# One pair of input chunks moved from chunk-wise products to block products, and the block-product pairs dealt out in another order

## The chip, the cores and the metric

The kernel runs on one core of a Trainium2 chip. The metric is the time of one execution on the device, in microseconds (us). Each kernel is executed several times and the median is given. One execution is taken by the hardware profiler; its records are called the trace here, and the page made from them the profile. Engines are named as in the profile: PE is the matrix engine (TensorE), PEld its weight loads, DVE VectorE, ACT ScalarE, POOL GpSimd, SP SyncE, which here only issues transfers. A difference of less than about 0.3% is not told from none.

## What is computed

One layer of a hybrid decoder trunk in float32, for 1024 positions and 1024 channels. The part of the reference that matters here:

```
h = rms_norm(x, g_mix)
z = einsum("bsd,de->bse", h, w_in) + b_in
va, ga, xb, gb, sa, sb = split(z)            # widths 1024 1024 1536 1536 1024 1024

u = va * sigmoid(ga)
u = causal_depthwise_conv(u, conv_a_w, conv_a_b)      # 31 taps
y_a = silu(layer_norm(u)) @ w_a_out

v = causal_depthwise_conv(xb, conv_b_w, conv_b_b)     # 4 taps
v = rg_lru(v, ...)                                    # gates by 16 heads, then a scan
y_b = (v * gelu(gb)) @ w_b_out

x = x + (sigmoid(sa) * y_a + sigmoid(sb) * y_b) @ w_o
x = x + square(relu(rms_norm(x, g_mlp) @ w_1)) @ w_2
return rms_norm(x, g_final)
```

## The kernel before

The 7168 output channels of `z` are 56 chunks of 128: VA and GA (8 each), XB and GB (12 each), SA and SB (8 each). All matmuls are float32 products made of three passes on 128x512 tiles: each operand is split into a high and a low part (`h`, `l`), and high by high, high by low and low by high are added up.

**First part (lines 735 and 836 to 897).** The list `CH` (line 694) names the chunks that are computed directly: 28 of them, all of VA, GA and XB. A chunk is 48 matmuls over the normalized input (`chunk_mm`). One loop runs over the chunks; at each step `s` it issues the load of the weights of chunk `s + 2`, the matmuls of chunk `s`, what follows from chunk `s - 1` (a bias and a convolution of XB, or `u_out`, which takes the sigmoid of GA on ACT and multiplies it by VA on DVE), and the weight splits of the next chunk (`split_w`: high part on ACT, low part by a POOL transfer that adds up). In between stand the head products of the recurrence (`head_mm`, tiles `rg`) and its scans in four groups (`scan_exp`, `scan_in`, `scan_root`, `scan_tile`), and the 31 taps of the convolution over each `u` (`conv`), which DVE does whenever it has nothing that is due. A finished convolution is stored (`yd`) and later summed over the eight tiles by POOL transfers (`ysum`).

Towards its end this part also prepares the second one: sums and differences of the four quarters of the input (`x_load`, `x_sum`, `x_parts`, lines 669 to 692), read back from a DRAM copy `xu`, and the first weights (`z_load`, tiles `zw`).

**Second part (lines 925 to 1063).** GB, SA and SB are computed in pairs of chunks. The input is cut into 2 x 2 blocks (channels by positions), the weights of a pair likewise, and seven block products give the four output blocks instead of eight (`z_mm`, 12 matmuls each, line 933). `ZPAIRS` (line 739) lists the 14 pairs: six of GB, four of SA, four of SB. `zseq` (line 785) gives the order of the products; the first two pairs are woven together, the others follow at seven products each. For each product a weight operand `zo` is made four products ahead (`z_lhs`: ACT and DVE, or ACT and a POOL transfer) from a block of `zw` or from a sum of blocks (`z_sums`, tiles `zs`). Behind the products stand the moves between banks (`z_post`) and the outputs (`z_out`): gelu on ACT for GB and a product with the scan's result `hb`, which goes to DRAM; a sigmoid on ACT for SA and SB, stored as `gates`.

**The rest.** `y_b`, layer norm, `y_a` and the output projection follow, in which the row statistics `x1_sums` and `x1_spread` use small banks of their own. Then the up projection by block products: the steps `gu` (line 1297) and `f` (line 1591) are woven by the table `GX` (line 1678), by numbered steps; the copy `u_late` (line 1351) takes the first sums of `gu4` and `gu5` out of their banks (`gu4a`, `gu5a`) before TensorE adds to them again. Last is the down projection (line 1903). All orders are fixed when the program is built: a list of clocks `clk` per engine is kept by hand (`at`, `later`, `vector_work`), and each engine runs its instructions in the order in which they were written.

Of the kernel before, what the change touches and what calls it, by code (L numbers as in the profile page):

```python
# [15 lines left out]
P = 128  # L16
# [15 lines left out]
def trunk_kernel(ctx: ExitStack, tc: tile.TileContext, x, xt_in, xt_eo, vecs, w_in, w_a_out, w_b_out,  # L32
# [87 lines left out]
    ep = stage.enter_context(tc.tile_pool(name="extra", bufs=1))  # L120
# [285 lines left out]
    xu = dp.tile([2, 4, P, S], F32, name="xu")  # L406
# [75 lines left out]
    def xb_parts(t):  # L482
        if t % 3 == 2:
# [67 lines left out]
    def scan_exp(g):  # L551
        at("A", 1.28)
        for t in range(3 * g, 3 * g + 3):
# [29 lines left out]
    def u_out(j, psv, psg):  # L583

        u = T(f"u{j}")
        uv = u.rearrange("p (o n) -> p o n", o=2)
        nc.scalar.activation(uv, psg.rearrange("p (n o) -> p o n", o=2), AF.Sigmoid,
                             bias=bin_c[:, GA + j:GA + j + 1])
        later(at("A", 1.11), 1.28, nc.vector.scalar_tensor_tensor, uv,
              psv.rearrange("p (n o) -> p o n", o=2), bin_c[:, VA + j:VA + j + 1], uv,  # L590
              ALU.add, ALU.mult)
        ut[j] = u
        fresh.append(j)
# [73 lines left out]
    xq = {}  # L667

    def x_load(c2):

        xq[c2] = {n: ep.tile([P, S], F32, tag="e", name=f"xs{n}_{c2}") if (n, c2) == (21, 0) else T(f"xs{n}_{c2}")
                  for n in (11, 12, 22, 21)}
        for n, a in xq[c2].items():
            nc.sync.dma_start(a, xu[n % 10 - 1, 2 * (n // 10 - 1) + c2])

    def x_sum(c2, ready):
        q = xq[c2]
        for n, a, b in ((11, 12, 11), (12, 22, 12), (22, 22, 11), (21, 21, 22)):
            later(ready, 1.2, nc.vector.tensor_tensor, q[n], q[a], q[b], ALU.subtract)

    def x_parts(c2, *ps):
        for p in ps:
            src = xq[c2][{6: 22, 7: 12, 5: 11, 4: 21}[p]]
            xbh[p][c2] = h = T(f"xs{p}h_{c2}", F32R)
            xbl[p][c2] = l = T(f"xs{p}l_{c2}", F32R)
            if c2 == 0 and p < 6:
                split_dma(src, h, l)
                at("A", 2.0)
            else:
                nc.scalar.activation(h, src, AF.Copy)  # L690
                later(at("A", 1.0), 1.2, nc.vector.tensor_tensor, l, src, h.bitcast(F32),
                      ALU.subtract)

    CH = [XB, VA, GA, XB + 1, XB + 2]
    for js, g in (((1,), 1), ((2,), 2), ((3,), 3), ((4, 5, 6, 7), 4)):
        CH += [c for j in js for c in (VA + j, GA + j)]
        CH += [XB + t for t in range(3 * g, min(3 * g + 3, 12))]
# [41 lines left out]
    ZPAIRS = [GB + 2 * i for i in range(6)] + [SA + 2 * i for i in range(4)]  # L739
    ZPAIRS += [SB + 2 * i for i in range(4)]  # L740
# [4 lines left out]
    def z_load(i, kk):  # L745

        zraw[i, kk] = raw = qp.tile([P, 2, 4, P], F32, tag="p", name=f"zw{i}_{kk}", bufs=4)
        c = ZPAIRS[i]
        nc.sync.dma_start(raw, w_in[c:c + 2, :, 4 * kk:4 * kk + 4, :].rearrange("m p k c -> p m k c"))
# [18 lines left out]

    def z_lhs(i, p):
# [12 lines left out]
        zo[i, p] = o  # L782
# [19 lines left out]
    HS0 = [4 + 5 * (n // 4) + n % 4 for n in range(NH)]  # L802
# [8 lines left out]
    for c2 in range(4):  # L811
        nc.sync.dma_start(xu[1, c2], xc[4 + c2])
    w_parts(3)
    with tc.manual_schedule(engines=ENGINES):
        for s in range(3, NC1):
            w_load(s + 2)
            if s in XL:
                x_load(XL[s])
# [19 lines left out]
            if before is not None:  # L838

                head_gate(before, 0, begun)  # L840
                head_mm(before, 1)
            if s > 3:
                chunk_mm(s, 18, 24)
            if new is not None:
# [3 lines left out]
            if c >= XB:  # L848
                xb_out(c - XB, zps[s - 1])
            elif c >= GA:  # L850
# [14 lines left out]
            for d in range(6):  # L865
                if s - d in EXP:
                    g = EXP[s - d]
                    lag = int(g < 3)
# [9 lines left out]
                    if 3 * g <= t < 3 * g + 3 and t < 11:  # L878
                        later(rooted[t], 4.8, scan_tile, t)
            if s == NC1 - 1:  # L880
                z_get(0, z_lhs)
                z_get(1, z_lhs)
            if s - 1 in XL:
                x_sum(XL[s - 1], max((r for r, *_ in todo), default=0))
            for f, *a in XS.get(s, ()):
                f(*a)
            if s == NC1 - 3:
                for i in range(4):
                    z_load(i // 2, i % 2)
            if s == 3:  # L890
                for c2 in range(4):
                    nc.sync.dma_start(xu[0, c2], xc[c2])
# [45 lines left out]
    def z_out(i, m_, hf, src, name):  # L938
        ci = ZPAIRS[i] + m_
        bias = bin_c[:, ci:ci + 1]  # L940
        if ci < SA:
# [17 lines left out]

    hb = {}  # L960

    def z_h(i, m_, hf):
        t = ZPAIRS[i] + m_ - GB
        if t < 12:
# [32 lines left out]
    ZX = {0: ((x_parts, 1, 7),), 7: ((later, 0, 4.8, scan_tile, 11),), 2: ((x_parts, 1, 5),), 4: ((x_parts, 1, 4),)}  # L997
    H_AT = {2: (0, 0), 5: (1, 1), 3: (0, 1), 4: (1, 0)}
    with tc.manual_schedule(engines=ENGINES):
# [40 lines left out]
        u_out(7, zps[NC1 - 2], zps[NC1 - 1])  # L1040
        x_parts(1, 6)
        vector_work(clk["V"])
        z_h(0, 0, 0)
        for n in range(len(zseq) + 2):
# [5 lines left out]
            taps["hold"] = n < 2  # L1050
# [372 lines left out]
    def x1_sums():  # L1423

        rst["ps"] = ps = bank("ssm")
# [48 lines left out]
    def x1_root(o):  # L1474
# [4 lines left out]
        if o == 0:  # L1479
            nc.vector.tensor_scalar(v, rst["ps"][:, 0:4], 1.0 / D, EPS, ALU.mult, ALU.add)  # L1480
# [19 lines left out]
    def x1_spread(o):  # L1500

        rd, rbk[o] = rbk[o], bank(f"rbm{o}")
# [146 lines left out]
    def g_get(n, f):  # L1649
# [500 lines left out]
```

## Time and profile before

| | |
|---|---|
| median of 3 runs | 1546.58 us (1546.01 to 1550.48) |
| profiled execution | 1546.4 us, span 1544.3 us, clock of TensorE 0.998 |
| first part, chunks from 42.63 us | until 360.62 us |
| second part, block products | from 360.62 us until about 630 us |
| last stage, down projection | from 1226.44 us |

The span is what the trace covers of the profiled execution. Starts are counted from its beginning. A row of the timeline gives start, length, engine, line, operation, output and input tiles with their shapes, and in brackets the idle time in front of it with the instruction that ended it. Matmuls overlap: one lasts 0.39 us in the trace, but the next starts 0.2267 us after it. A row of the order of instructions (fences in the next section) has the line, the operation, output and input tile, with numbers that tell tiles of one name apart.

### The profile page before, as it was taken

What the parts mean: (1) busy time and instruction counts of PE and PEld (TensorE: products, weight loads), DVE (VectorE), ACT (ScalarE), POOL (GpSimd) and SP (SyncE); (2) the same over time, 40 slices, a digit from 0 to 9 for tenths busy, and PEclk for the clock granted to TensorE, in tenths of its full rate; (3) what the DMA queues carried; (4) which work ended last, traced back from release to release, by engine and by line L of the source; (5) the groups of instructions that cost most, each with busy time, mean ns of one, the idle gap of its engine ahead of it and who ended that gap; (6) DMA issues with size and microseconds to landing.
All of it is one profiled execution on the core that took longest, in us unless ns stands there. A gap on an engine that the chain in (4) does not pass through costs nothing.

```text
span 1544.3 us, 19039 instructions
## 1 busy us (share of the span) xinstructions
PE 1533.0 (99%) x6777; PEld 1261.0 (82%) x6777; DVE 1218.4 (79%) x1643; ACT 903.5 (59%) x1258; POOL 188.6 (12%) x226
## 2 busy tenths in 40 slices
PE   9999999999999999999999999999999999999998
PEld 7878888788888888888888887888888888888886
DVE  6999989999899983468568878765555558888897
ACT  6748677576657657435275777444444475555553
POOL 0000000002222222000022332000000001111110
PEclk9999999999999999999999999999999999999999
DMA  8653654678999889854579897523333779888852
GB/s 348 169 127 94 161 139 134 155 229 218 263 263 260 196 204 259 278 191 122 185 198 302 192 195 190 205 80 134 116 114 109 242 205 228 224 224 223 206 125 109
DMA packets 132815, 294.18 MB, mean 190 GB/s; under 512 B 20848, under 2 KB 38896, under 8 KB 132720
## 3 DMA queue, kind: packets, MB, share of 16 engines
q1 hardware_dynamic: 101184, 213.00, 41.1%
q0 software_dynamic: 31392, 79.71, 28.2%
q8 instruction: 53, 0.87, 0.2%
q14 instruction: 42, 0.34, 0.1%
q10 hardware_dynamic: 144, 0.26, 0.1%
HBM read 152.93 MB, written 58.72 MB: 137 GB/s over the span
## 4 chain that ended last, share of the span: by engine, by line
PE 98%; DMA 1%; DVE 0%; ACT 0%; issue 0%; DVEq 0%; SPq 0%; POOL 0%; POOLq 0%
PE z L735 18%; PE d L1903 15%; PE yb L1121 8%; PE e L2020 3%; PE keep L1903 2%; PE z L258 2%; PE rg L530 1%; PE rg L532 1%; PE rg L531 1%; DMA zo<-zs 1%; PE gu5a L1297 0%; PE go2e L1297 0%; PE z5a L933 0%; PE gu3a L1297 0%; PE gu1a L1297 0%; PE go0e L1297 0%
## 5 line engine op out<-in xcount | busy, mean ns | idle before, releaser
L735 PE MATMUL z<-xh,win_h 128*128 128x512 f32 x400 | 124.8, 390 | 0.0
L735 PE MATMUL z<-xl,win_h 128*128 128x512 f32 x400 | 123.4, 389 | 0.0
L1915 DVE TENSOR_TENSOR acc<-acc,d 128x1024 f32<-128x1024 f32 x72 | 87.9, 1220 | 33.3 <-PE d L1903 32.7
L735 PE MATMUL z<-xh,win_l 128*128 128x512 f32 x400 | 99.4, 391 | 0.0
L735 PEld LDWEIGHTS z<-xh,win_l 128*128 128x128 f32 x400 | 75.1, 188 | 16.9
L735 PEld LDWEIGHTS z<-xh,win_h 128*128 128x128 f32 x400 | 75.0, 188 | 16.6 <-ACT win_h L68 0.4
L648 DVE SCALAR_TENSOR_TENSOR y<-u,vec,y 128x511 f32<-128x511 f32 (+14 forms) x120 | 88.5, 737 | 0.0
L735 PEld LDWEIGHTS z<-xl,win_h 128*128 128x128 f32 x400 | 75.1, 188 | 15.8
L648 DVE SCALAR_TENSOR_TENSOR yt<-u,vec,yt 128x511 f32<-128x511 f32 (+6 forms) x112 | 82.7, 738 | 0.0
L648 DVE SCALAR_TENSOR_TENSOR y<-yt,csum,y 128x511 f32<-128x511 f32 (+6 forms) x112 | 82.7, 738 | 0.0
L542 ACT ACTIVATE g<-rg,vec 96x1024 f32<-96x1024 f32 x32 | 35.6, 1113 | 79.6 <-PE rg L532 79.5
L1579 ACT ACTIVATE o<-s 128x512 fp32r<-128x512 f32 x58 | 34.7, 623 | 51.7 <-DVE s L1564 31.0
L67 POOL DMA_DIRECT2D win_l<-win_raw x25 | 21.6, 865 | 318.9 <-ACT win_l L66 248.4
L476 DVE SCALAR_TENSOR_TENSOR v<-xb,vec,v 128x1023 f32<-128x1023 f32 (+2 forms) x36 | 46.2, 1282 | 11.4 <-ACT v L467 10.4
L67 POOL DMA_DIRECT2D zo<-zw x42 | 36.2, 862 | 133.1 <-ACT zo L66 126.2
L1121 PE MATMUL yb<-hgh,wb_h 128*128 128x512 f32 x168 | 51.7, 389 | 0.0
L1121 PE MATMUL yb<-hgl,wb_h 128*128 128x512 f32 x168 | 51.7, 389 | 0.0
L66 ACT ACTIVATE zo<-zw 128x512 fp32r<-128x512 f32 x42 | 26.3, 626 | 31.0 <-DMA zw<-in_w_in_dram 8.9
L67 POOL DMA_DIRECT2D db_1l<-wr x7 | 6.0, 860 | 309.9 <-ACT db_1l L66 287.3
L1121 PE MATMUL yb<-hgh,wb_l 128*128 128x512 f32 x168 | 41.0, 389 | 0.0
L1085 DVE TENSOR_TENSOR o<-s,o 128x512 fp32r<-128x512 f32 x58 | 38.8, 683 | 0.0
L1121 PEld LDWEIGHTS yb<-hgh,wb_h 128*128 128x128 f32 x168 | 31.5, 188 | 6.6
(1795 smaller groups left out, 4667.5 us busy)
## 6 DMA issues: line engine op xcount, KB each, us to landing
w_raw<-in_w_dram SPq DMA_DIRECT2D x36, 512.0 KB, 5.6
fr<-fd SPq DMA_DIRECT2D x32, 512.0 KB, 6.0
wr<-in_w_dram SPq DMA_DIRECT2D x32, 512.0 KB, 6.1
zw<-in_w_in_dram SPq DMA_DIRECT2D x28, 512.0 KB, 6.1
win_raw<-in_w_in_dram SPq DMA_DIRECT2D x25, 512.0 KB, 4.1
win_l<-win_raw POOLq DMA_DIRECT2D x25, 512.0 KB, 4.5
zo<-zw POOLq DMA_DIRECT2D x42, 256.0 KB, 5.7
gates<-zg SPq DMA_DIRECT2D x32, 256.0 KB, 3.9
```

The lines of the kernel that those rows point to most:

```text
L67: nc.gpsimd.dma_start(l, src, accum_op=ALU.add)
L258: nc.tensor.matmul(z0[i][:, HALVES[hf]], w0[i][w][:, k, :], xpart(a, hf, k), start=k == 0 and which == "hh", stop=k == 7 and which == ("hl ...
L476: nc.vector.scalar_tensor_tensor(v[:, d:S], a[:, 0:S - d], cbw_c[:, w * 12 + t:w * 12 + t + 1], v[:, d:S], ALU.mult, ALU.add)
L542: nc.scalar.activation(a, gps.pop((n, gi))[:HD, :], AF.Sigmoid, bias=(ba_c, bx_c)[gi][:, n:n + 1])
L648: nc.vector.scalar_tensor_tensor(o[:, k:], a[:, 0:HS - k], c, o[:, k:], ALU.mult, add)
L735: nc.tensor.matmul(zps[s][:, HALVES[hf]], w[:, k, :], xw[k][part][hf], start=n == 0, stop=n == 23)
L1085: tt(l, src, h.bitcast(F32), ALU.subtract)
L1121: nc.tensor.matmul(ps[hf], a, b[:, HALVES[hf]], start=n == 0, stop=n == len(todo) - 1)
L1579: nc.scalar.activation(o[:, 0], src, AF.Copy)
L1903: nc.tensor.matmul(o, a, b, start=n == 0 and (p != 1 or g == 0), stop=n == len(todo) - 1, skip_group_check=p == 1 and g > 0)
L1915: tt(acc[p, q2], acc[p, q2], ps, ALU.add)
L2020: nc.tensor.matmul(o, a, b, start=n == 0 and t < 7, stop=n == len(todo) - 1, skip_group_check=t == 7)
```

## The change

One pair of chunks, VA 7 and GA 7, leaves the first part and becomes the pair `u7` of the second part. So `CH` has 26 chunks and is written out, its last two in the order GA 6, VA 6: the sigmoid of GA 6 is taken while VA 6 is multiplied, for which `u_out` is cut into `u_gate` and `u_value`. The pairs, 15 now, are dealt out: two SA, three GB, two SA, `u7`, three GB, four SB. `z_branch` and `z_joined` make `u7` out of the pair's four output blocks, and only then its convolution can begin.

The sums of the input quarters are no longer read back and made at the end of the first part. They are made in place in its steps 4 to 7 (`x_sum`), split or left whole (`x_make`), and stored in `xsd`. Before and early in the second part they are loaded (`x_get`, `x_raw`), and those left whole are split there (`x_split`, products 2, 3, 6 and 7). The last group of scans starts two steps ahead of the part's end, and its three tiles are scanned at the products 1, 4 and 9 of the second part; taps are held back for six products there instead of two. The first weights of the second part are loaded at step 24 of the 26. The low part of a `zo` is made on DVE for all products once the convolutions are over. In `GX` the operands for product 7 of `gu` come a step later, those for product 3 in one step. `x1_sums` uses the bank `rbm0` of the first `x1_spread`. Tiles of one small pool (`extra`) go to others.

The core of the diff:

```diff
-    CH = [XB, VA, GA, XB + 1, XB + 2]
-    for js, g in (((1,), 1), ((2,), 2), ((3,), 3), ((4, 5, 6, 7), 4)):
...
+    NJ = 7
+    CH = [XB + 0, VA + 0, GA + 0, XB + 1, XB + 2, VA + 1, GA + 1, XB + 3, XB + 4, XB + 5, VA + 2, GA + 2, XB + 6, XB + 7, XB + 8, VA + 3, GA + 3, XB + 9, XB + 10, XB + 11, VA + 4, GA + 4, VA + 5, GA + 5, GA + 6, VA + 6]
...
-    ZPAIRS = [GB + 2 * i for i in range(6)] + [SA + 2 * i for i in range(4)]
-    ZPAIRS += [SB + 2 * i for i in range(4)]
+    ZPAIRS = [{"u": lambda i: (VA + i, GA + i)}.get(
+        t[0], lambda i, c={"g": GB, "s": SA, "t": SB}.get(t[0]): (c + 2 * i, c + 2 * i + 1))(int(t[1]))
+        for t in "s0 s1 g0 g1 g2 s2 s3 u7 g3 g4 g5 t0 t1 t2 t3".split()]
...
-        if p in (7, 5):
+        if p in (7, 5) or conv_over():
...
-    EXP = {head_slot: g for g, head_slot in enumerate(HS0[4 * g + 3] + 1 for g in range(4))}
-    XL = {23: 0, 25: 1}
-    XS = {25: ((x_parts, 0, 6),), 26: ((x_parts, 0, 7, 5),), 27: ((x_parts, 0, 4),)}
+    EXP = {head_slot: g for g, head_slot in enumerate(HS0[4 * g + 3] + 1 for g in range(3))}
+    RAW = (4, 5)
+    XS = {4: ((x_sum, 0),), 5: ((x_make, 0, 5), (x_make, 0, 7)), 6: ((x_make, 0, 6), (x_make, 0, 4), (x_sum, 1)),
+          7: tuple((x_make, 1, p) for p in (5, 7, 6, 4)),
+          NC1 - 3: ((scan_exp, 3),), NC1 - 2: ((x_get, 0, 6), (x_get, 1, 6)),
+          NC1 - 1: ((scan_in, 0, 9, 10, 11), (scan_root, 3), (x_get, 0, 7), (x_get, 1, 7))}
...
-        if ci < SA:
+        if ci < XB:
+            z_branch(ci, hf, src, bias)
+        elif ci < SA:
...
+    def z_branch(ci, hf, src, bias):
+        j = ci % GA
+        if j not in zu:
+            zu[j] = T(f"u{j}")
+        d, g = halved(zu[j], hf), src.rearrange("p (n o) -> p o n", o=2)
+        if ci >= GA:
+            zg[j, hf] = g
+            nc.scalar.activation(src, src, AF.Sigmoid, bias=bias)
+            ready = at("A", 0.62)
+            if hf == 0:
+                later(ready, 0.63, nc.vector.tensor_tensor, d, d, g, ALU.mult)
+                z_joined(j)
+        elif hf == 0:
+            nc.scalar.activation(d, g, AF.Identity, bias=bias)
+            at("A", 0.62)
+        else:
+            later(0, 0.68, nc.vector.scalar_tensor_tensor, d, g, bias, zg.pop((j, hf)), ALU.add, ALU.mult)
+            z_joined(j)
...
-    ZX = {0: ((x_parts, 1, 7),), 7: ((later, 0, 4.8, scan_tile, 11),), 2: ((x_parts, 1, 5),), 4: ((x_parts, 1, 4),)}
+    ZX = {0: ((x_raw, 0, 5), (x_raw, 1, 5)), 1: ((later, 0, 4.8, scan_tile, 9),), 2: ((x_split, 0, 5),), 3: ((x_split, 1, 5),),
+          4: ((later, 0, 4.8, scan_tile, 10), (x_raw, 0, 4), (x_raw, 1, 4)), 6: ((x_split, 0, 4),), 7: ((x_split, 1, 4),),
+          9: ((later, 0, 4.8, scan_tile, 11),)}
...
-            taps["hold"] = n < 2
+            taps["hold"] = n < 6
...
-        8: ((g_parts, "u", 7, 0),), 9: ((up_lhs, 0, 7), (g_parts, "u", 7, 1), (up_lhs, 1, 7)),
-        10: ((g_parts, "u", 3, 0), (g_t, "u", 0, 4)),
-        11: ((g_parts, "u", 3, 1), (g_t, "u", 1, 4))}.items()})
+        9: ((g_parts, "u", 7, 0), (up_lhs, 0, 7)), 10: ((g_parts, "u", 7, 1), (up_lhs, 1, 7)),
+        11: ((g_parts, "u", 3, 0), (g_t, "u", 0, 4), (g_parts, "u", 3, 1), (g_t, "u", 1, 4))}.items()})
```

What the order of instructions shows at the places that matter. First PE in the up projection, where `f1b` (a bank of the step `f`) and the second addition to the bank `gu4a` meet; before:

```order
L1591 MATMUL f0b_8097<-gu6h1_7947,o0_6_7922 128x512
L1591 MATMUL f1b_8115<-gu6h0_7913,o1_6_7956 128x512
L1591 MATMUL f1b_8115<-gu6l0_7914,o1_6_7956 128x512
L1591 MATMUL f1b_8115<-gu6h0_7913,o1_6_7956 128x512 x2
L1591 MATMUL f1b_8115<-gu6l0_7914,o1_6_7956 128x512
L1591 MATMUL f1b_8115<-gu6h0_7913,o1_6_7956 128x512
L1591 MATMUL f1b_8115<-gu6h1_7947,o1_6_7956 128x512
L1591 MATMUL f1b_8115<-gu6l1_7948,o1_6_7956 128x512
L1591 MATMUL f1b_8115<-gu6h1_7947,o1_6_7956 128x512 x2
L1591 MATMUL f1b_8115<-gu6l1_7948,o1_6_7956 128x512
L1591 MATMUL f1b_8115<-gu6h1_7947,o1_6_7956 128x512
L1297 MATMUL gu4a_8003<-gu2h0_7653,gu4_2_7943 128x512
```

and of the change:

```order
L1635 MATMUL f0b_8117<-gu6h1_7967,o0_6_7942 128x512
L1635 MATMUL f1b_8135<-gu6h0_7933,o1_6_7976 128x512
L1635 MATMUL f1b_8135<-gu6l0_7934,o1_6_7976 128x512
L1635 MATMUL f1b_8135<-gu6h0_7933,o1_6_7976 128x512 x2
L1635 MATMUL f1b_8135<-gu6l0_7934,o1_6_7976 128x512
L1341 MATMUL gu4a_8023<-gu2h0_7673,gu4_2_7963 128x512
```

Gu4a now comes after 5 matmuls of f1b, not after all 12. Its other 11 follow, then the 12 of gu5a, and only then the 7 left of f1b; before, gu5a stood behind 9 matmuls of f0c.

The same place on ACT: `f11` is an output of `gu`, `gu7h` a high part for product 7, `o` a weight operand of `f` made of the sum `s3` of DVE, and `u1_late` the copy for which gu4a and gu5a wait. Before:

```order
L1356 ACTIVATE f11_3_7999<-gu3a_7846 128x512
L1239 ACTIVATE gu7h0_8016<-x1010_7493 128x1024
L1351 ACTIVATE u1_late_8020<-gu4a_8003 128x512
L66 ACTIVATE o0_7_8037<-s3_0_8035 128x512
L68 ACTIVATE o0_7_8037<-s3_0_8035 128x512
L1239 ACTIVATE gu7h1_8041<-x1011_7529 128x1024
L66 ACTIVATE o1_7_8046<-s3_1_8044 128x512
L68 ACTIVATE o1_7_8046<-s3_1_8044 128x512
L1351 ACTIVATE u1_late_8020<-gu5a_8022 128x512
```

and of the change:

```order
L1400 ACTIVATE f11_3_8019<-gu3a_7866 128x512
L1395 ACTIVATE u1_late_8036<-gu4a_8023 128x512
L1283 ACTIVATE gu7h0_8051<-x1010_7514 128x1024
L66 ACTIVATE o0_7_8056<-s3_0_8054 128x512
L68 ACTIVATE o0_7_8056<-s3_0_8054 128x512
L1395 ACTIVATE u1_late_8036<-gu5a_8038 128x512
L1283 ACTIVATE gu7h1_8074<-x1011_7550 128x1024
```

Between f11 and the second u1_late stand one gu7h and two `o` where there were two and four, and nothing stands ahead of the first.

Last the queue of SP at the end of the first part: `hd` are scan results on their way out, `win` raw weights of a chunk, `xs` and `xb` sums of the input, `zw` raw weights of the first two pairs. Before:

```order
L577 DMA hd_446<-g1_8_1974 128x1024
L61 DMA win26_raw_2595<-in_w_in_dram 128x1024
L656 DMA yd_447<-y3_2071 128x1024
L61 DMA win27_raw_2678<-in_w_in_dram 128x1024
L674 DMA xs11_1_2680<-xu_445 128x1024
L674 DMA xs12_1_2681<-xu_445 128x1024
L674 DMA xs22_1_2682<-xu_445 128x1024
L674 DMA xs21_1_2683<-xu_445 128x1024
L749 DMA zw0_0_2745<-in_w_in_dram 128x2x512
L749 DMA zw0_1_2747<-in_w_in_dram 128x2x512
```

and of the change:

```order
L61 DMA win25_raw_2494<-in_w_in_dram 128x1024
L577 DMA hd_443<-g1_8_1972 128x1024
L764 DMA zw0_0_2638<-in_w_in_dram 128x2x512
L764 DMA zw0_1_2640<-in_w_in_dram 128x2x512
L764 DMA zw1_0_2642<-in_w_in_dram 128x2x512
L764 DMA zw1_1_2644<-in_w_in_dram 128x2x512
L698 DMA xb6h_0_2646<-xsd_442 128x1024
L698 DMA xb6l_0_2648<-xsd_442 128x1024
L698 DMA xb6h_1_2650<-xsd_442 128x1024
L698 DMA xb6l_1_2652<-xsd_442 128x1024
L698 DMA xb7h_0_2732<-xsd_442 128x1024
```

The zw loads stand straight behind hd of tile 8, ahead of the sums; before, two chunk weights, a convolution's result and four sums stood in between.

More of the change, by code (lines that the diff above doesn't have):

```diff
@@ L403, in trunk_kernel @@
                 first_z(i, 1, k, "lh")
-    xu = dp.tile([2, 4, P, S], F32, name="xu")
+    xsd = dp.tile([4, 2, 2, P, S], F32, name="xsd")
     def first_scale(i):
@@ L549, in trunk_kernel, with scan_exp @@
     at_, rooted = {}, {}
-    def scan_exp(g):
-        at("A", 1.28)
-        for t in range(3 * g, 3 * g + 3):
+    def scan_exp(g, part=range(3)):
+        if 0 in part:
+            at("A", 1.28)
+        for t in (3 * g + n for n in part):
             r = gate[0, t]
@@ L665, in trunk_kernel @@
         xbh[p], xbl[p] = [None, None], [None, None]
[L667 to L692, printed above, removed]
@@ new lines, in trunk_kernel, with x_store, x_get, x_raw @@
+    stored = []
+    def x_store():
+        for a in stored:
+            nc.sync.dma_start(*a)
+        stored.clear()
+    def x_get(c2, p):
+        for n, a in enumerate((xbh, xbl)):
+            a[p][c2] = T(f"xb{p}{'hl'[n]}_{c2}", F32R)
+            nc.sync.dma_start(a[p][c2].bitcast(F32), xsd[p - 4, c2, n])
+    def x_raw(c2, p):
+        xbl[p][c2] = T(f"xb{p}l_{c2}", F32R)
+        nc.sync.dma_start(xbl[p][c2].bitcast(F32), xsd[p - 4, c2, 0])
+    def x_split(c2, p):
+        xbh[p][c2], l = T(f"xb{p}h_{c2}", F32R), xbl[p][c2]
+        nc.scalar.activation(xbh[p][c2], l.bitcast(F32), AF.Copy)
+        later(at("A", 1.06), 1.2, nc.vector.tensor_tensor, l, l.bitcast(F32), xbh[p][c2].bitcast(F32),
+              ALU.subtract)
@@ L767, in z_sums, with conv_over @@
             S_(4, z_blk(i, 0, 1), zs[i, 2], ALU.subtract)
+    def conv_over():
+        return not (ut or fresh or taps["wait"] or taps["now"] or taps["next"])
     def z_lhs(i, p):
@@ L1423, in x1_sums @@
     def x1_sums():
-        rst["ps"] = ps = bank("ssm")
+        rbk["row"] = ps = bank("rbm0")
         for n in range(4):
@@ L1500, in x1_spread @@
     def x1_spread(o):
-        rd, rbk[o] = rbk[o], bank(f"rbm{o}")
+        rd, rbk[o] = rbk[o], rbk["row"] if o == 0 else bank(f"rbm{o}")
         for i in range(4):
```

84 lines of the change are left out of this document (48 added, 36 removed).

## The prediction

> **What bounds the kernel now.** First the head of the page: the span, the busy time of the engines, and by which engine the chain that ended last was held.
>
> ```profile
> span 1544.3 us, 19039 instructions
> PE 1533.0 (99%) x6777; PEld 1261.0 (82%) x6777; DVE 1218.4 (79%) x1643; ACT 903.5 (59%) x1258; POOL 188.6 (12%) x226
> PE 98%; DMA 1%; DVE 0%; ACT 0%; issue 0%; DVEq 0%; SPq 0%; POOL 0%; POOLq 0%
> ```
>
> TensorE is busy for 99% of the span and is 98% of the chain. So the time is the number of matmuls by their spacing, and the stalls. The spacing is read from the chain in order of time, in its runs of one line:
>
> ```profile
> 42.63 21.76 PE z L735 x96
> ...
> 470.19 2.72 PE z6a L933 x12
> 472.92 2.72 PE z6f L933 x12
> ...
> 478.36 2.72 PE z6b L933 x12
> ```
>
> Two chunks of the first part (2 x 48 matmuls) are one row of 21.76 us, 0.2267 us a matmul. A block product of the second part, 12 matmuls, is 2.72 us, the same spacing. The products follow each other without a hole (470.19 + 2.72 is 472.91).
>
> Then the stalls, in the waits of TensorE (engine, line <- whom it waited for: total us, times, longest):
>
> ```profile
> PE keep L1903 <- DVE fb L1626: 0.9, 1, 0.9
> PE gu5a L1297 <- ACT u_late L1351: 0.9, 1, 0.9
> PE gu4a L1297 <- ACT u_late L1351: 0.3, 1, 0.3
> ```
>
> They are small: what an edit frees on another engine can't return more than these few tenths. Only fewer matmuls, or a new stall, can move the time by more.
>
> **The matmuls.** VA 7 and GA 7 leave the first part: two chunks, 96 matmuls, the 21.76 us of the row above. They return as the pair u7, seven products of 2.72 us, 84 matmuls, 19.04 us. That is 19.04 - 21.76 = **-2.72 us**. The order of the changed program has 12 of those matmuls fewer and no other kind changed, so this term is sure. The products need no new kind of operation: 15 pairs where there were 14.
>
> **The up projection.** Two stalls stand there, and the change moves rows on both engines. PE first, then ACT, from the timeline (start, length, what, and in brackets the idle time before it with its releaser):
>
> ```profile
> 951.45 0.39 PE L1591 MATMUL f1b<-gu6h,o 128*128 128x512 f32 x1
> 952.09 0.50 PE L1297 MATMUL gu4a<-gu2h,gu 128*128 128x512 f32 x1 [0.25 <-ACT u_late L1351]
> ...
> 956.78 0.39 PE L1591 MATMUL f0c<-gu5h,o 128*128 128x512 f32 x1
> 958.03 0.50 PE L1297 MATMUL gu5a<-gu2h,gu 128*128 128x512 f32 x1 [0.87 <-ACT u_late L1351]
> ```
>
> ```profile
> 950.03 0.59 ACT L1356 ACTIVATE f<-gu3a 128x512 f32<-128x512 f32 x1
> 950.50 1.05 ACT L1239 ACTIVATE gu7h<-x 128x1024 fp32r<-128x1024 f32 x1
> 951.45 0.58 ACT L1351 ACTIVATE u_late<-gu4a 128x512 f32<-128x512 f32 x1
> 954.36 0.63 ACT L66 ACTIVATE o<-s 128x512 fp32r<-128x512 f32 x1 [2.32 <-DVE s L1567]
> ...
> 957.41 0.57 ACT L1351 ACTIVATE u_late<-gu5a 128x512 f32<-128x512 f32 x1
> ```
>
> From start to start, less one spacing of 0.23, they cost 0.41 and 1.02 us, together 1.43. In the new order ACT does the u_late copy of gu4a straight after f: it starts at 950.50 instead of 951.45 and ends at 951.08. By itself that would take the first stall away. But TensorE's order moves as well: gu4a comes after 5 matmuls of f1b instead of 12, at 951.45 - 6 x 0.2267 = 950.09, and waits till some 951.14, 1.05 us with the same spacing taken off. Gu5a now comes right behind gu4a's 12 (which ran from 952.09 to 954.97 before, 2.88), at 951.14 + 2.88 = 954.02. Its copy has two `o` copies ahead of it, which wait for the tile s of DVE:
>
> ```profile
> 951.30 0.68 DVE L1408 TENSOR_TENSOR f<-f 128x512 f32<-128x512 f32 x1
> ...
> 953.64 1.29 DVE L1567 TENSOR_TENSOR s<-w_raw,w_raw 128x512 f32<-128x512 f32 x2
> ```
>
> In the new order of DVE s comes straight after that f, not behind u and gu7l: it is ready about 952.6, the two `o` end the wait at 953.7, and u_late ends at 954.3: a stall of 0.3. Together 1.35 against 1.43, so I take **0**. The bounds: if s is no earlier than the 954.36 of the row, u_late ends at 956.0 and the second stall is 2.0 (+1.6 in sum); if both stalls go, -1.43.
>
> **The order in which pairs are dealt out.** ScalarE loads a table when the function changes between sigmoid and gelu. Before, all gelu pairs came first; now there are four changes. The order of ACT has 11 loads in the second part instead of 4, and one less in the first. What a load does, from ACT around the one change of before (pair 5 to pair 6):
>
> ```profile
> 472.95 0.58 ACT L971 ACTIVATE z6b<-z6a 128x512 f32<-128x512 f32 x1 [1.04 <-PE z6a L933]
> ...
> 483.35 1.28 ACT L956 ACT_TABLE_LOAD   x1
> 484.64 0.69 ACT L956 ACTIVATE zg<-z6a,vec 128x512 f32<-128x512 f32 x1
> ...
> 486.60 1.28 ACT L945 ACT_TABLE_LOAD   x1 [0.22 <-PE z5e L933]
> ```
>
> A load is 1.28 us and the next activation starts as it ends. Seven more are 7 x 1.28 = 9.0 us of ACT. They lie beside TensorE if the copy that TensorE needs next has that much room: z6a ends at 472.91, its copy to z6b is ready at 472.95 + 0.58 = 473.53, and z6b's product starts at 478.36: 4.83 us of room, against 1.28. The chain's rows above show no hole around these loads. ACT has the time as well:
>
> ```profile
> 360.62:626.90 266.28, 266.19 (x1175) 219.87 (x1174) 222.36 (x333) 177.24 (x297) 64.79 (x76) 1.00 0.94 238
> 560.00:680.00 120.00, 120.00 (x531) 99.33 (x530) 62.85 (x84) 64.62 (x99) 14.70 (x17) 1.00 0.86 252
> ```
>
> In these rows of the windows the busy times are PE, PEld, DVE, ACT, POOL, then the clock and the DMA share. ACT is busy for 177.24 of 266.28 us in the second part. What could still be late are split weights (zo), whose low part goes over a POOL transfer of its own. One such stall is there:
>
> ```profile
> 414.51 0.89 POOL L607 DMA_DIRECT2D ysum<-yd  x1
> 417.46 0.88 POOL L67 DMA_DIRECT2D zo<-zs  x1 [2.06 <-ACT zo L66]
> ...
> 426.19 0.39 PE L933 MATMUL z2e<-xl,zo 128*128 128x512 f32 x1
> 426.67 0.73 PE L933 MATMUL z2e<-xh,zo 128*128 128x512 f32 x2
> ```
>
> The transfer was issued at 417.46 behind a ysum load, and the product that needs it waited until 426.67: 0.48 less 0.23 of spacing, and 0.12 in the next matmul (0.57 for two, with 0.45 usual), 0.37 in all. The bounds for four changes instead of one are 0 (as at pair 6) and 9.0 (every new load in front of TensorE). I take the price of one more such stall, **+0.4**, since the nearest rows are the ones without a hole.
>
> The Trainium skill's page "ScalarE: Activation LUTs", section "What ACT_TABLE_LOAD costs", gives a load about 1.28 us and a drain of about 1.38 us more for each switch to another set; by it seven loads would be an estimated 18.6 us of ACT. The trace agrees with the first figure and not with the second: the activation behind the load at 483.35 starts 1.29 later.
>
> **The start of the second part.** Its first weights (zw) and input sums now come from loads issued about three chunks ahead:
>
> ```profile
> 309.43 0.32 SPq L577 DMA_DIRECT2D hd<-g  x1
> ...
> 333.88 2.07 SPq L749 DMA_DIRECT2D zw<-in_w_in_dram  x4
> zw<-in_w_in_dram SPq DMA_DIRECT2D x28, 512.0 KB, 6.1
> ```
>
> Before, zw was issued at 333.88 for a part that starts 360.62. Now it stands on SP behind hd of group 8, which left at 309.43, for a start at 360.62 - 21.76 = 338.86: 29 us, where 27 were enough. The eight loads of sums behind it go in part into tiles that the last chunk still reads (its 48 matmuls would run from 327.98 to 338.86, and it reads them until about 332), so they land some 6 to 9 us later (the 6.1 of the row, or 9.2 as a slow zo transfer above), 338 to 341. The first four products don't read them; the fifth, 10.9 us into the part, is the first, at 349.7. I take **0**. Bounds: 0 to +3 if one of them is late by a product.
>
> **The input sums early, and the rest.** Eight sums and their splits move from the end of the first part to its chunks 4 to 7. The nearest rows are
>
> ```profile
> 363.44 1.22 DVE L453 TENSOR_TENSOR xs6l<-xs,xs6h 128x1024 fp32r<-128x1024 f32 x1
> 364.10 1.04 ACT L690 ACTIVATE xs7h<-xs 128x1024 fp32r<-128x1024 f32 x1
> 83.30:97.10 13.80, 13.80 (x62) 11.02 (x61) 13.80 (x23) 5.18 (x6) 0.46 (x1) 1.00 0.60 148
> ```
>
> Twelve DVE operations of 1.22 are 14.6 us, four ACT copies 4.2 us, four of the stores are issued by ACT and eight by SP. ACT is busy 5.18 of 13.80 us in the window of these chunks, DMA 0.60. DVE is full, 13.80 of 13.80, but with the taps of the convolutions, which TensorE reads only much later. So the taps go back, and with the later u7 the last convolution ends later. The cover:
>
> ```profile
> 575.51 0.34 SPq L656 DMA_DIRECT2D yd<-y  x1
> 648.56 1.23 DVE L1085 TENSOR_TENSOR ysuml<-ysum,ysumh 128x1024 fp32r<-128x1024 f32 x1 [0.19 <-ACT ysumh L1159]
> ```
>
> The last convolution leaves at 575.51, its sum is used at 648.56, and DVE is busy only 62.85 of 120.00 us between 560 and 680 (row above). Some 20 us later is still inside the 70 us of cover; without it the taps would cost their own time. **0.** The first-part stall on win_h and the one ahead of `keep` have the same neighbours in the new order: 0. The bank that the row statistics now share (rbm0) is waited for by nobody in the waits of TensorE: 0.
>
> **Sum.** The profiled execution took 1546.4 us, 1544.3 of it the span; the median of the runs, 1546.58, is 0.2 above it. 1546.4 - 2.72 + 0 + 0.4 + 0 = **1544.1 us**, -0.15%.
>
> **Rivals.** A change of 0.3% is 4.64 us, about what a measurement of this kernel can tell from no change: faster means under 1541.8, slower over 1551.0.
>
> *Faster.* The dealt-out order spreads the transfers, and the stalls go that stand in the rows: u_late 1.43, zo 0.37. For it: their copies come earlier in ACT's order. Against: gu4a comes earlier as well. 1546.4 - 2.72 - 1.43 - 0.37 = 1541.9, a hair short of the bound; with a second zo stall it is 1541.5.
>
> *The saving is spent at the start.* The loads of sums and the pair's weights meet in one queue, SP, behind hd of scan tiles that DVE now makes inside the second part. For it: they are issued in a stretch of few us. Against: 29 us for zw. One late product is 2.72 us: 1546.8; it decides from one product on, and stays within the bound until three.
>
> *Slower.* The seven table loads stand ahead of copies that TensorE waits for: 7 x 1.28 = 9.0, so 1544.1 - 0.4 + 9.0 = 1552.7. The place is ACT at the changes between gelu and sigmoid pairs. It decides from 7.3 us of new stalls, that is from six of the seven loads. For it: at a change two kinds of pair finish side by side, so that loads come close together (483.35 and 486.60 above). Against: 4.83 us of room and no hole at 483 to 488. The Trainium skill's page "ScalarE: Activation LUTs", section "Table sets: the hidden batching unit", speaks against dealing out: it treats the set as the unit in which such work is to be batched, all of one before the next.
>
> *The change doesn't do what it says.* The order shows 12 matmuls fewer, so only a stall of 2.7 us just where they went could hide it: 1546.4.
>
> **Chances.** Forecast 0.46 (own range 1543.0 to 1546.0), faster 0.10, spent at the start 0.22, slower 0.20, nothing 0.02. Of the faster case 0.08 lies under 1541.8, of the others nearly all within the bound: faster 0.08, same 0.72, slower 0.20. The range reaches from 1541.5 to 1553.0, which takes in the slower case's price.
>
> **What would show it.** PE with 12 fewer 128x512 matmuls, and the second part starting 21.8 us earlier, near 338.9, with 15 x 7 products at 2.72, the last of them 2.7 us earlier than before. In the waits of TensorE: u_late with about 1.3 in all, zo <- POOL with one or two of some tenths. ACT's table loads at 1.28 with no PE idle behind them. Wrong would be: PE idle over 1 us between 338 and 390 (loads of sums, zw), PE waiting for ACT copies z.b at the pairs s1/g0, g2/s2, u7/g3, g5/t0, PE waiting for ysum after 640, or stalls in the first part's chunks 4 to 9.

## The result and the profile after

| | before | after |
|---|---|---|
| median | 1546.58 us (9 runs) | 1542.07 us (9 runs, 1541.17 to 1543.75) |
| ratio | | 0.9969 (95% interval 0.996 to 0.9978) |
| profiled execution, span | 1546.4, 1544.3 us | 1542.07, 1540.3 us |

The changed kernel is 0.31% faster. That is the sign that was forecast, at the edge of the bound of 0.3%, and inside the whole range (1541.5 to 1553.0). But it is 4.3 us between the two profiled executions where 2.3 were forecast, and 0.9 us below the 1543.0 to 1546.0 that the forecast case itself had. The head of the page of the changed kernel:

```profile
span 1540.3 us, 19049 instructions
PE 1530.1 (99%) x6765; PEld 1258.2 (82%) x6765; DVE 1228.9 (80%) x1660; ACT 911.2 (59%) x1270; POOL 184.7 (12%) x221
```

TensorE has 12 matmuls fewer (6777 to 6765) and 2.9 us less to do. Its chain in order of time, at the places that the prediction quoted:

```profile
43.20 21.76 PE z L749 x96
...
339.39 2.72 PE z0a L948 x12
...
448.76 2.72 PE z6a L948 x12
```

The spacing is the same: 21.76 us for two chunks, 2.72 for a block product. Against the rows of before the first chunk starts 0.57 us later (42.63 to 43.20), the second part 21.23 us earlier (360.62 to 339.39), and the pair numbered 6 21.43 us earlier (470.19 to 448.76). The waits of TensorE:

```profile
PE spare L344 <- POOL ones L114: 1.6, 1, 1.6
PE gu4a L1341 <- ACT u_late L1395: 0.6, 1, 0.6
PE z L257 <- ACT xh L226: 0.4, 2, 0.2
PE z L257 <- DVE xl L230: 0.2, 1, 0.2
```

The row of `keep` is gone, and that of gu5a; the row of `spare`, at the very start, is the same in every profile here. A place in the program where the shift between the two traces changes is a place where time was won or lost. The first three rows are starts of pieces of the chain above, the others starts of the first matmul in the timeline of PE; both kernels are read in the same way:

| stage | before | after | shift | step |
|---|---|---|---|---|
| first chunk of the loop | 42.63 | 43.20 | +0.57 | start: +0.57 |
| first block product | 360.62 | 339.39 | -21.23 | two chunks fewer: -21.8 |
| pair 6 | 470.19 | 448.76 | -21.43 | stalls of zo: -0.2 |
| `yb` | 622.35 | 619.96 | -2.39 | seven products more: +19.04 |
| `gu4a`, first time | 940.80 | 938.42 | -2.38 | 0 |
| `f1c` | 961.57 | 958.70 | -2.87 | u_late: -0.49 |
| `d`, behind `keep` | 1231.96 | 1227.97 | -3.99 | keep: -1.12 |

Behind `d` nothing moves any more; the last 0.3 of the 4.33 us lie outside the span (1546.4 less 1544.3 is 2.1, 1542.07 less 1540.3 is 1.8).

The stall that went, from the timeline of PE and DVE, first before:

```profile
1225.18 0.39 PE L1591 MATMUL f15d<-gu4h,o 128*128 128x512 f32 x1
1226.44 0.47 PE L1903 MATMUL keep<-db_1h,da_1h 128*128 128x512 f32 x1 [0.88 <-DVE fb L1626]
```

```profile
1225.60 0.69 DVE L1626 TENSOR_TENSOR fb<-f15d,u 128x512 f32<-128x512 f32 x1 [0.23 <-PE f15d L1591]
```

and after:

```profile
1222.31 0.39 PE L1635 MATMUL f15d<-gu4h,o 128*128 128x512 f32 x1
1222.54 0.39 PE L1946 MATMUL keep<-db_1h,da_1h 128*128 128x512 f32 x1
```

```profile
1222.73 0.69 DVE L1670 TENSOR_TENSOR fb<-f15d,u 128x512 f32<-128x512 f32 x1 [0.22 <-PE f15d L1635]
```

Before, `keep` stands still until DVE has read f15d out of its bank. After, it follows f15d by one spacing (0.23) and runs while DVE still reads. DVE comes just as late in both, 0.42 us behind the start of f15d's last matmul: so it was not DVE that became earlier.

### The profile page after: what moved, and what is told of

Read it like the earlier page. It is cut to its first block, busy times and chain, and to the rows that moved or that the text cites. A ratio compares the mean times of both kernels' runs of the same rounds, so it can differ in the third digit from the quotient of the medians.

```text
span 1540.3 us, 19049 instructions
## 1 busy us (share of the span) xinstructions
PE 1530.1 (99%) x6765; PEld 1258.2 (82%) x6765; DVE 1228.9 (80%) x1660; ACT 911.2 (59%) x1270; POOL 184.7 (12%) x221
## 3 DMA queue, kind: packets, MB, share of 16 engines
q10 hardware_dynamic: 720, 2.36, 0.4%
## 4 chain that ended last, share of the span: by engine, by line
PE 97%; DMA 1%; ACT 1%; DVE 1%; issue 0%; SPq 0%; POOL 0%; DVEq 0%; POOLq 0%; ACTq 0%
PE z L749 16%; PE d L1946 15%; PE yb L1165 8%; PE e L2063 3%; PE keep L1946 2%; PE z L257 2%; PE rg L529 1%; PE rg L531 1%; PE rg L530 1%; DMA w_raw<-in_w_dram 1%; DMA xc<-in_xt_dram 0%; PE z4a L948 0%; PE go2e L1341 0%; PE z4e L948 0%; PE z2e L948 0%; PE z3e L948 0%
## 5 line engine op out<-in xcount | busy, mean ns | idle before, releaser
L749 PE MATMUL z<-xh,win_h 128*128 128x512 f32 x368 | 115.0, 390 | 0.0
L749 PE MATMUL z<-xl,win_h 128*128 128x512 f32 x368 | 113.5, 389 | 0.0
L749 PE MATMUL z<-xh,win_l 128*128 128x512 f32 x368 | 91.8, 391 | 0.0
L749 PEld LDWEIGHTS z<-xh,win_l 128*128 128x128 f32 x368 | 69.1, 188 | 15.6
L749 PEld LDWEIGHTS z<-xh,win_h 128*128 128x128 f32 x368 | 69.0, 188 | 15.3 <-ACT win_h L68 0.4
L749 PEld LDWEIGHTS z<-xl,win_h 128*128 128x128 f32 x368 | 69.1, 188 | 14.6
L1172 DVE TENSOR_TENSOR sb<-yb,sb 128x512 f32<-128x512 f32 x16 | 10.3, 685 | 34.4 <-PE yb L1165 34.4
```

Of the source, the lines that this page charges most:

```text
L749: nc.tensor.matmul(zps[s][:, HALVES[hf]], w[:, k, :], xw[k][part][hf], start=n == 0, stop=n == 23)
```

## The experiments

Times are medians beside runs of the kernel before on the same chip. Theory and rival are told at each.

**The measure (e5).** The changed kernel once more, beside e6 to e8.

> The changed kernel unchanged, on the chip of the runs beside it, as their measure. All theories: 1542.1, give or take 0.5. What this run adds: its profile shows how much of the two stalls at gu4a and gu5a (1.17 us in the first profile, 1.77 and 1.94 in those of e2 and e4 with the same table) and of the stalls at the start (0.6 to 1.7 us in the four profiles) varies from execution to execution. Theory (load): the stall at gu4a follows the landing of the raw weight load that ACT waits for at about 930 us, by some 0.6 us for each us that it lands later.

Measured: 1542.27 us, ratio 0.9968 (0.9956 to 0.9979). Its profile has a stall of zo at z2e (0.97 with the matmul behind it) that the first one hasn't, and 1.36 at u_late. So single stalls of some tenths come and go, and differences of 0.5 us between two of these kernels are not shown by one profile.

**The banks (e1, e2).** Theory: tiles take one of eight banks after the other, so the number of tiles taken decides which tile meets which bank later. In e1 the kernel before takes over only this:

```diff
-        rst["ps"] = ps = bank("ssm")
+        rbk["row"] = ps = bank("rbm0")
```

> The kernel before, with one edit of the change alone: x1_sums uses the bank rbm0 of the first x1_spread instead of a bank of its own. Theory (banks): banks are dealt out in rotation, so one bank less shifts all later ones by one; the first tile of the down projection (keep) then no longer falls on the bank that the last product of the up projection (f15d) used, and its stall of 1.04 us and the 0.08 behind it at 1225 us goes. About 1545.5 us against 1546.6 of the kernel before (-1.1), with no keep row in the waits of PE and both u_late rows as they were. Rival (timing): the stall went because the vector work ahead of it came earlier through the other edits; then this kernel stays at 1546.6 with the keep stall of 1.0.

Measured: 1546.0 us, ratio 0.9997 (0.9988 to 1.0005), where 1545.5 was expected. The waits of PE in its profile:

```profile
PE spare L345 <- POOL ones L114: 1.6, 1, 1.6
PE z L258 <- ACT xh L227: 1.1, 1, 1.1
PE gu5a L1297 <- ACT u_late L1351: 0.9, 1, 0.9
PE z4a L933 <- DMA zo<-zw: 0.5, 1, 0.5
PE z0b L933 <- DMA zo<-zs: 0.4, 1, 0.4
PE z L258 <- DVE xl L231: 0.2, 1, 0.2
```

The row of keep is gone, with nothing else edited: the mechanism is shown. Of the two u_late rows, which were to stay, only gu5a is in the list; at gu4a TensorE still loses 0.26 us, before 0.41. The gain in time is not shown, since stalls of zo (0.65 and 0.77 us with the matmul behind each) stood in this profile in its place and the interval is wider than the effect. E2 undoes the same edit in the changed kernel.

> The changed kernel with this one edit undone: x1_sums has a bank of its own again. Theory (banks): the keep stall of about 1.1 us is back at about 1222.5 us, 1543.2 against 1542.1 of the changed kernel. Rival (timing): no keep stall, 1542.1.

Measured: 1542.76 us, ratio 0.9974 (0.9962 to 0.9985), and no keep stall:

```profile
1222.89 0.39 PE L1635 MATMUL f15d<-gu4h,o 128*128 128x512 f32 x1
1223.11 0.39 PE L1946 MATMUL keep<-db_1h,da_1h 128*128 128x512 f32 x1
```

The expectation missed: the pair u7 takes four banks more, and with it f15d's bank is away from keep already. In the program's order the wait for DVE's reading of f15d now stands ahead of the first `d` tile, behind both tiles of keep. The programs as built tell where it lies: the two tiles of keep take banks 0 to 3 and those of `d` 4 to 7; f15d is in bank 0 before, in 2 in e1, in 4 in e2 and in 7 after the change (and in e3, so the table doesn't move it). Of all the kernels here only before, e9 and e10 have it in bank 0, and only their profiles have the row of keep. So one bank fewer does it, three more do it, and four more do it as well; of these counts only that of before hit. The theory of e1, that one bank less shifts all later ones by one, is too simple: f15d moved by two. The rival (DVE earlier) fails by the rows above.

**The table of the up projection (e3, e7, e10).** E3 puts the old table of steps back into the changed kernel.

> The changed kernel with the table of the up projection as it was before. If the new table is worth what the two profiles differ by at the u_late waits (1.66 us lost before, 1.17 after), this kernel is 0.5 us slower than the changed one, 1542.6, with the two stalls of 0.41 and 1.03 at gu4a and gu5a again. Rival: the stalls come from what ACT and DVE still have to do there and hardly change with the table: within 0.2 us of 1542.1.

Measured: 1542.62 us, ratio 0.9973 (0.9962 to 0.9984), with stalls of 0.68 and 0.95 us. That looked like the theory, till the profiles were put side by side. ACT waits there for a raw weight from DRAM; before and after:

```profile
930.12 0.60 ACT L1351 ACTIVATE u<-gu3a 128x512 f32<-128x512 f32 x1 [2.19 <-PE gu3a L1297]
933.13 0.63 ACT L66 ACTIVATE gu<-w_raw 128x512 fp32r<-128x512 f32 x1 [2.42 <-DMA w_raw<-in_w_dram]
```

```profile
927.74 0.60 ACT L1395 ACTIVATE u<-gu3a 128x512 f32<-128x512 f32 x1 [2.19 <-PE gu3a L1341]
930.07 0.63 ACT L66 ACTIVATE gu<-w_raw 128x512 fp32r<-128x512 f32 x1 [1.74 <-DMA w_raw<-in_w_dram]
```

From the start of the one row to that of the other are 3.01 us before and 2.33 after. Over the profiles, that distance and what TensorE then lost at gu4a and gu5a (with the matmul behind each):

| | distance and loss, us |
|---|---|
| new table | 2.33 and 1.17 (after), 2.36 and 1.36 (e5), 2.43 and 1.31 (e6), 3.05 and 1.72 (e8), 3.12 and 1.92 (e12), 3.39 and 1.77 (e2), 3.64 and 1.94 (e4) |
| old table | 2.20 and 1.33 (e9), 2.81 and 1.56 (e1), 3.01 and 1.66 (before), 3.49 and 1.86 (e3) |

Each us that the weight is later costs about 0.5, and at one distance the two tables can't be told apart: the losses scatter by 0.2 with one table. Of the -0.49 some 0.34 (0.5 times the 0.68 between the two distances, an estimate) was the landing of one load; the rest is within that scatter, and nothing is left that the table would have to explain. E7 sends that load out ahead of four stores in SP's queue:

```diff
-        0: ((x1_rows, 4, 5, 6, 7),), 1: ((up_load, 4, (0,)), (up_load, 0, (1,))),
+        0: ((up_load, 4, (0,)), (x1_rows, 4, 5, 6, 7)), 1: ((up_load, 0, (1,)),),
```

> The changed kernel with one weight load of the up projection (raw weights of row block 8, for gu4) issued ahead of four stores of the normalized rows in SP's queue instead of behind them. Theory (load): ACT's wait for it at about 930 us goes, its work there comes 2 to 3 us earlier, u_late is ready before TensorE comes to gu4a and gu5a, and the stalls of 1.2 to 1.9 us go: about 1540.7 (-1.4 against the changed kernel). Rival (table): the stalls come from the order of the table alone and stay: 1542.1; or the stores that now come later hold up what reads them, and the time is the same or some tenths longer.

Measured: 1541.51 us, ratio 0.9971 (0.9962 to 0.998). The waits of PE in its profile:

```profile
PE spare L344 <- POOL ones L114: 1.6, 1, 1.6
PE z2e L948 <- DMA zo<-zs: 0.4, 1, 0.4
PE z L257 <- ACT xh L226: 0.4, 1, 0.4
PE z L257 <- DVE xl L230: 0.2, 1, 0.2
PE gu1a L1341 <- DMA gu<-w_raw: 0.2, 1, 0.2
```

Both u_late rows are gone, and a small one is there for another weight. The mechanism holds; that the kernel is faster than the changed one (1542.27 beside it, ratio 0.9968) isn't shown: the intervals overlap, and by the ratio it isn't even ahead. The same edit in the kernel before is e10.

> The kernel before with the weight load of row block 8 of the up projection ahead of the stores of the normalized rows, as in e7, nothing else. Theory (load): ACT's wait at about 933 us goes, and of the 1.66 us at gu4a and gu5a a part; ACT still does two more pieces ahead of u_late there, so 0.5 to 1.4 us: 1545.2 to 1546.1. Rival: the old table keeps both stalls: 1546.6.

Measured: 1547.35 us, ratio 1.0006 (0.9997 to 1.0015), with gu4a waiting 1.0 and gu5a 0.8. Neither theory: the wait moved on to the next weight,

```profile
940.95 0.63 ACT L66 ACTIVATE gu<-w_raw 128x512 fp32r<-128x512 f32 x1 [6.59 <-DMA w_raw<-in_w_dram]
```

6.59 us on ACT, and u_late is as late as ever. In e7 ACT took the same weight at 934.79, where the changed kernel took it at 935.29. So what the edit wins hangs on the load after it too; why that one was late in e10, its one profile doesn't tell.

**The order of the pairs (e4, e8, e12, e6, e9).** E4 goes back to gelu first in the changed kernel:

```diff
-        for t in "s0 s1 g0 g1 g2 s2 s3 u7 g3 g4 g5 t0 t1 t2 t3".split()]
+        for t in "g0 g1 g2 g3 g4 g5 s0 u7 s1 s2 s3 t0 t1 t2 t3".split()]
```

> The changed kernel with the pairs in one run of gelu and one of sigmoid: g0 to g5, s0, u7, s1 to s3, t0 to t3. ACT then loads 4 tables fewer or more in that part. Theory (loads and transfers hidden): the seven loads of the dealt-out order cost nothing, and the transfers of the gelu pairs lie closer again, so that stalls of zo of 0.3 to 0.5 us come back: 1542.3 to 1542.6. Rival (loads on the path): each new load of 1.28 us that TensorE had to wait for is won back, up to 1542.1 - 9.0; anything under 1541.5 would speak for it. Second rival: the later u7 lets its convolution end too late, with a wait for ysum after 640 us; then some us slower.

Measured: 1546.68 us, ratio 0.9996 (0.9987 to 1.0005): the whole gain is gone. It has seven table loads fewer and is 4.4 us slower, so nothing is won back from the loads; and there is no wait for ysum after 640 us. Pieces of its chain of waits:

```profile
377.89 8.98 DMA zo<-zs
...
396.97 11.58 DMA zo<-zs
```

These two zo transfers took 9.0 and 11.6 us, and TensorE stood still at z1e (1.3), z3a (1.5), z2e (1.2) and z4a (0.4, each with the matmul behind it), 4.3 us in all. The first ended the wait at z1e, the second that at z2e. Is it that gelu pairs, with their loads and stores of scan results, come while the input sums are still being loaded, or that six stand in a row? E8 keeps the six in a row, behind s0, s1 and u7.

> The changed kernel with s0, s1 and u7 first, then the six gelu pairs in one run, then s2, s3 and the four t. It tells apart what the old order (e4, 1546.7) lost by. Theory (start): the gelu pairs' transfers collide with the loads of input sums and scan results at the start of the second part; with three sigmoid pairs first the loads are over, and the time is that of the changed kernel, 1542.1 to 1542.8. Rival (run): six gelu pairs in a row keep the transfers too dense wherever they stand, so stalls of zo of 3 to 4 us come, 1545 to 1546.5, now some 57 us later.

Measured: 1542.61 us, ratio 0.997 (0.9959 to 0.9982), one zo stall of 0.34. Six in a row are harmless there. What else stands at the start is seen in POOL's queue of e4:

```profile
393.79 0.86 POOL L67 DMA_DIRECT2D zo<-zw  x1 [1.91 <-ACT zo L66]
394.33 0.88 POOL L612 DMA_DIRECT2D ysum<-yd  x1
396.97 0.85 POOL L67 DMA_DIRECT2D zo<-zs  x1 [1.77 <-ACT zo L66]
```

Between two zo stands the first sum of a finished convolution, 512 KB, on the same queue. The zo ahead of it was late as well: it is the one for which z3a waits, and it took 10.9 us from its issue at 393.79.

```profile
404.71 0.73 PE L948 MATMUL z3a<-xh,zo 128*128 128x512 f32 x2 [1.18 <-DMA zo<-zw]
```

So "a zo behind a ysum is late" says too little: the one 0.54 us ahead of the sum is late with it. E12 is e4 with these sums issued later:

```diff
-            if n >= 20 and n % 6 == 2:
+            if n >= 56 and n % 6 == 2:
```

> The kernel of e4 (the changed kernel with the old order of pairs, 1546.7) with the first sums of finished convolutions (ysum, POOL) issued from product 56 on instead of 20. In e4 the stalls at z3a, z2e and z4a (2.7 us with the matmul behind each) come just after a ysum load, at zo transfers that take 10 to 12 us; the one at z1e (1.3 us) comes before the first ysum. Theory (ysum): the two kinds of transfer share POOL's queue, and a zo behind a ysum is late; without it these three stalls go and z1e stays: 1544.0. Rival (density): the loads and stores of the gelu pairs are what makes zo slow, whatever else is queued: stalls of 3.5 to 4.3 us as in e4, 1546 to 1546.7.

Measured: 1543.47 us, ratio 0.9974 (0.9963 to 0.9984), against 0.9996 of e4. Its waits of PE:

```profile
PE spare L344 <- POOL ones L114: 1.6, 1, 1.6
PE gu4a L1341 <- ACT u_late L1395: 1.2, 1, 1.2
PE z L257 <- ACT xh L226: 0.9, 1, 0.9
PE gu5a L1341 <- ACT u_late L1395: 0.2, 1, 0.2
```

No zo row is left in it, with the gelu pairs still first. The median of zo<-zs from issue to landing between 360 and 460 us is 8.5 us in e4 and 7.1 here. The two zo around the place of the first sum took 10.9 and 11.6 us in e4, 8.7 and 8.2 here without the sum, and with the sum 7.6 each in the changed kernel and 8.5 and 8.3 in e8. So at that place both are needed, the gelu pairs first and the sum, and the sums are the larger part of the 4.4 us (3.2 of it are back in e12). It isn't so everywhere: in e8 the next sum, at 409.22, stands among gelu pairs too, the zo behind it takes 9.8 us, and TensorE loses no more than the 0.34. What else the first 60 us of the part hold, loads of input sums and scan results, was not taken out by itself. The stall at z1e, which comes ahead of any sum, was not expected to go and did; this one profile doesn't tell why.

E6 has the kinds of pairs in turn, for the table loads.

> The changed kernel with gelu and sigmoid pairs in turn: s0 g0 s1 g1 s2 g2 u7 g3 s3 g4 t0 g5 t1 t2 t3. That is eleven changes of kind instead of four, so some 20 more table loads of 1.28 us on ACT. Theory (loads are hidden): no PE idle behind them and the time of the changed kernel, 1542.1 give or take 0.6; stalls of zo no more than there. Rival (loads on the path): some of the loads come ahead of copies that TensorE waits for; one in three of 20 would be +8 us, 1550.

Measured: 1542.53 us, ratio 0.997 (0.9959 to 0.9982). ACT's loads in it, by line:

```profile
L973 ACT ACT_TABLE_LOAD x16 | 20.5, 1283 | 0.8 <-issue 0.5
L962 ACT ACT_TABLE_LOAD x16 | 20.5, 1283 | 3.2 <-PE z3e L948 0.5 <-PE z11a L948 0.5 <-PE z5a L948 0.5
```

These 32 loads (one more, at L986, makes 33) are 41 us of ACT where the changed kernel has 11 loads. The medians differ by 0.3 us, less than the noise. The traces say it more closely: from the first matmul of z0a to that of `yb` TensorE takes 280.75 us, and 280.74 in the changed kernel. So the loads lie beside TensorE here. The Trainium skill's page "ScalarE: Activation LUTs", section "Table sets: the hidden batching unit", would batch the calls by set. Its section "What ACT_TABLE_LOAD costs" adds a drain of about 1.38 us to each load; the trace doesn't agree, as behind each of the 33 the next activation starts 1.29 or 1.30 us after the load's start. E9 deals out the pairs in the kernel before.

> The kernel before with its 14 pairs dealt out as in the change (s0 s1 g0 g1 g2 s2 s3 g3 g4 g5 t0 to t3), nothing else. Theory (start): dealing out alone takes away the stalls of zo that the kernel before has in its second part (0.5 us in its first profile, 1.4 us in that of e1), and no more, since its input sums are in place before the part begins: 1545.8 (-0.3 to -1.2). Rival: dealing out is worth the same 4.6 us here as between e4 and the changed kernel: 1542. Second rival: the table loads cost something without the other edits: above 1547.

Measured: 1549.01 us, ratio 1.0015 (1.0006 to 1.0024), slower by 0.15%: the interval lies above 1, though the difference is under the bound of 0.3%. Its trace agrees: from z0a to `yb` it takes 264.94 us, where the three kernels with the old order and 14 pairs take 261.89 (before), 262.83 (e1) and 262.57 (e10). Only the second rival had the sign. Its chain of waits, at two places (pieces are left out):

```profile
411.01 1.28 ACT L956
...
418.91 9.12 DMA zo<-zs
...
434.80 10.12 DMA zo<-zw
```

```profile
533.94 10.10 DMA zo<-zs
```

The sums were issued at 415.87, 432.90 and 531.29, each 2 to 3 us ahead of one of these zo. The kernel before sent the first of the three out at 417.46, 1.45 us earlier; here a table load of 1.28 stands in the chain ahead of it. So one table load is on the path of one of the four stalls of zo (z3a, z2e, z4a and z8e, 3.4 us with the matmul behind each), and the rival's reason holds for a part at most; that is read from the chain and not tested by itself. The changed kernel, with the same order of pairs and its transfers at other times, doesn't show it.

**Both together (e11).** The order of e8 with the load of e7.

> The changed kernel with both edits that the runs point to: the order of e8 (s0 s1 u7, then six gelu pairs) and the early weight load of e7. Theory: the gain of e7 (-0.8) stays and the order is worth 0 give or take 0.4: 1541.5, below the kernel before by 5.0 and below the changed one by 0.7. Rival: with gelu pairs in a row the second part has more zo stalls and the gain is used up: 1542.2 or more.

Measured: 1542.48 us, ratio 0.9972 (0.996 to 0.9983). The rival: gu1a waits 0.9 us for another weight, zo stalls add 0.8. No version here is shown to beat the changed kernel.

## Why the prediction was right in sign and short by half

- **The matmuls** (-2.72): right. -21.8 and +19.04 between the stages.
- **The stall ahead of keep** (0, "the same neighbours in the new order"): this step failed, and is the largest part of the gap: -1.12. The neighbours are the same; the bank is not. The prediction looked for who waits for the shared bank, and not for what one bank fewer, or four more, does to later tiles. E1 shows it, and the bank of f15d in every kernel agrees (e2).
- **The up projection** (0, bounds -1.43 to +1.6): -0.49 in the profile. The working of both orders was right in its result: over the eleven profiles above nothing of a gain by the table can be told. It had stalls of 1.05 at gu4a and 0.3 at gu5a; the profile has 0.75 and 0.20. What it took as fixed, ACT's times, hangs on the landing of a weight, which varies by over 1 us.
- **The order of the pairs** (+0.4): -0.2. That table loads have room was right (e6), the added zo stall didn't come in this profile (e5 has one of 0.97). The -0.2 itself isn't told from none: e1 and e10, with the second part of before, take 0.9 and 0.7 us more for it than before did. But it was weighed as a cost only. With the rest of the change the old order costs 4.4 us (e4), of which the first sums of convolutions are the larger part (e12). The rival "slower" fails: seven loads, and 22 more, left TensorE's time as it was. The rival "faster" gave 1541.9, next to the 1542.07 measured, and that is luck: it had u_late and zo go wholly, 1.43 and 0.37, of which 0.49 and 0.2 went, and not the keep stall.
- **The start of the second part, the sums, the taps** (0): right. No PE wait between 339.39 and 390, and none after 640 for ysum.
- **The start of the kernel**: +0.57, not in the sum. It is no part of the change: in e5, the same program, the first matmul of the loop starts at 42.60, and in all the other profiles of either kernel between 42.43 and 42.74; only in this one is it 43.04.

Forecast -2.3; measured -4.3, of which -1.12 the bank, -0.49 the up projection (mostly the weight), -0.6 the order (from +0.4 to -0.2), +0.57 the start and -0.3 outside the span make the difference of -2.0.

## What to carry to other kernels

Where tiles go round over a few banks, an edit that takes one bank more or fewer can move the later meetings of tiles with banks: look through the waits of all later stages, not only that place. A transfer that must land within a few products shares its queue with whatever else is issued there: count the large ones that are issued just ahead of it or just behind it, and move those that have time. An order is worth what it is worth among the transfers of its own kernel: the same dealing out was worth 4.4 us in one kernel and lost some 2 in the other.

## What the runs showed of the hardware

Table loads on ACT, 33 of them at 1.283 us within the 285 us of the second part, left TensorE's time from its first product to `yb` as it was (280.75 us in e6, 280.74 in the changed kernel). Transfers of 256 KB that add up on POOL's queue and were issued 2 to 3 us behind one of 512 KB took 9.1 to 11.6 us where TensorE waited for them (e4, e9); the median was 7.1 without the large ones (e12), and 7.0 with them in the changed kernel. One that was issued 0.54 us ahead of the large one took 10.9 us (e4), so the order of the queue is not the whole reason. What is, the shared transfer engines or something else, stays open.
